# A second normalized-token tile in the router's stage of a two-layer encoder

## The chip, the cores and the metric

The kernel runs on one core of a Trainium2 chip. Its time is the device time of one execution in microseconds (us); smaller is better. The core's engines are named as the profile names them: PE (matrix multiply), DVE (vector), ACT (activations), POOL (general), and SP, which here only issues DMAs. DMAs that SP and ACT issue run on the same 16 DMA engines.

## The reference

Two layers over 512 tokens of 1,024 features. A layer is a mixer (a short convolution in the first, a gated linear recurrence in the second), a mixture of 32 experts with two experts for each token, and a gated embedding. Cut to what the change touches:

```python
h = h + mix                                    # the mixer's output projection ends here
xn = rmsnorm(h, norm_ffn[i])                   # y * g, y = h * rsqrt(mean(h*h) + EPS)
h = h + hier_moe(xn, ...)
# hier_moe:
pg = softmax(xn @ w_rg + b_rg); g_top = argmax(pg)          # 4 groups
le = (xn @ w_re + b_re) of the group g_top                  # 8 experts each
top_p, top_i = top_k(softmax(le), 2)                        # 2 experts a token
y = sum over the token's experts of weight * (silu(x @ w_gate[e]) * (x @ w_up[e])) @ w_down[e]
```

## The kernel before

Tokens lie in four tiles t = 0..3 of 128. Everything is built in an order written out by hand: each engine runs its instructions in the order in which the code issues them, and waits only for semaphores. A small queue, `Flow`, holds functions that are due some ticks later; the loops over the matrix multiplies tick it, so the router's steps for a tile are laid between the multiplies of the following tiles.

The mixer ends with `out_proj`, which finishes the tiles in the order 0 to 3. For each, `to_moe` adds the projection to `h` (L1323), and queues: the transposes for the router (`turn`, L762), its logits (L771), `norm`, `rest`, `ranks` and `weights`, and last `pull`. The steps that matter here:

- `norm(t)` makes the normalized tokens `xn` in two DVE instructions (L473); ACT copies them into the high part `X.hi` (L1336) and issues the write of `xn` to the DRAM table `xs` (L1337, 512 KB), from which later expert pairs gather rows.
- `rest(t)` makes the low part `X.lo` (L1341, DVE, two instructions, tile `x_z`).
- `ranks(t)` counts a token's place in its expert (PE L800 and L801, DVE L802), and DVE marks the places of the first four experts in `R` (L834, `hot`).
- `pull(t, p)` multiplies `R` with the high (p = 0) or low (p = 1) part (PE L830, eight matmuls each), and so gathers the tokens of the first four experts.

The four results of the pulls are copied to `xt` (ACT L944, DVE L942), and `gate_up(0)` starts the experts (PE L985). `leave` then frees the tiles of `X`, which become homes of weight loads. `Loader` issues all weight loads on SP in the order of use (L73), each as soon as a home is free; an expert's gate and up weights come in loads of 512 KB, its down weights in loads of 1 MB, 384 MB in both layers. A plain DMA's end is counted on one of eight semaphores (DMAHW0 to DMAHW7), and a new DMA on a semaphore waits until the last one there has ended.

The tile `xn` comes from the pool `bnd`, which is open while `out_proj` runs. The number of buffers is `bnd["xn"]`, 1 here. With one buffer, `norm(t)` must wait until the write of tile t - 1 to `xs` has read it to its end. When `bnd` closes, the space goes to `xt` and the experts' small tiles.

Of the kernel before, what the change touches and what calls it, by code (L numbers as in the profile page):

```python
# [10 lines left out]
F32 = mybir.dt.float32  # L11
F32R = mybir.dt.float32r
BF = mybir.dt.bfloat16
F16 = mybir.dt.float16
# [3 lines left out]
ALU = mybir.AluOpType  # L18
# [3 lines left out]
P = 128  # L22
# [3 lines left out]
KD = D // P  # L26
NG = 4
EPG = 8
NE = NG * EPG
# [4 lines left out]
OB = 128  # L34
# [195 lines left out]
def hybrid_encoder(ctx, tc, A, out):  # L230
    nc = tc.nc
    ctx.enter_context(tc.manual_schedule())

    def pool(name, bufs=1, side=None):
        return tc.tile_pool(name=name, bufs=bufs, side=side, reuse_waits="tile")
# [3 lines left out]
    bnd = {}  # L239
    small = ctx.enter_context(pool("small", 2))  # L240

    def homes(p, n, tag):
        return [(p, "%s%d" % (tag, j)) for j in range(n)]

    base = homes(ctx.enter_context(pool("base")), BASE, "base")
# [5 lines left out]
    def aux(shape, dt=F32):  # L251
        return psum.tile(shape, dt, name="aux", tag="aux", bufs=3)
# [116 lines left out]
    def iota(name, shape, dt=F32, **kw):  # L369
        t = const.tile(shape, dt, name=name)  # L370
        early.append(lambda: nc.gpsimd.iota(t, allow_small_or_imprecise_dtypes=True, **kw))
        return t
# [4 lines left out]
    nc.vector.memset(mhalf, -0.5)  # L377
    minus = const.tile([P, 1], F32, name="minus")
    nc.vector.memset(minus, -1.0)
    slot1 = iota("slot1", [P, OB], pattern=[[1, OB]], base=1, channel_multiplier=0)  # L380
    tok1 = iota("tok1", [P, S], F16, pattern=[[1, S]], base=-AWAY, channel_multiplier=0)
    tokp = iota("tokp", [P, T], pattern=[[P, T]], base=-AWAY, channel_multiplier=1)
    ovi = iota("ovi", [P, NOV], pattern=[[1, NOV]], base=0, channel_multiplier=0)
# [13 lines left out]
    gffn = [chan[:, P + i * KD:P + (i + 1) * KD] for i in range(2)]  # L397
# [163 lines left out]
    def out_proj(after):  # L561
        pss = [acc([P, 512]) for _ in range(T)]
        for j in range(4):
            wh, wl = W.take()
            for t in range(T):
                for kk in range(2):
                    k = 2 * j + kk
                    three(pss[t], X.h(t, k), X.l(t, k), wh[:, kk], wl[:, kk], k == 0, k == KD - 1)
                flow.tick()
            W.done()  # L570
            W.pump()
        for t in range(T):
            after(t, 0, pss[t])
        ws = [W.take() for _ in range(4)]
        for t in range(T):
            ps = acc([P, 512])
            token_group(ps, t, ws, lambda: after(t, 1, ps))
        W.done(4)

    def out_stage(i, Z, old, start, after):  # L580
        nonlocal X
        X = Z
        spare = bnd["spare"] = ExitStack()
        L.open(homes(spare.enter_context(pool("spare", 1, "right" if i else "left")), 1, "spare"), moe_end[i] + 4)
        with pool("bnd", 1, "right") as bnd["pool"]:
            bnd["xn"] = 1
            start()
            W.widen(old)
            spent = []

            def spend(at):
                if at in old:
                    return
                spent.append(at)
                L.open([at], moe_end[i] - 4 if len(spent) < WSP else None)

            W.spent = spend
            out_proj(after)
            assert len(spent) == WSP
            flow.drain()  # L600

    def mix_a(start, after):
        Z = Split(zhome)
        with pool("mixt", 2, "right") as mt:
            for q in range(4):
# [18 lines left out]
                for j in range(2):  # L624
# [4 lines left out]
                    split_z(Z, u, ft)  # L629
                    W.pump()  # L630
        out_stage(0, Z, xhome, start, after)
        xst.close()

    def mix_b(start, after):
# [91 lines left out]
        for ft in range(KD):  # L726
# [5 lines left out]
            W.pump()  # L732
        hs.close()
        out_stage(1, Z, zhome, start, after)
        zst.close()

    def router_load(i):
        wr = bnd["pool"].tile([P, KD, 40], F32, name="wr", tag="wr", bufs=1)
        st = bnd["pool"].tile([P, KD * 36], F32, name="wrs", tag="wrs", bufs=1)
        gv, ev = [st[:, a:b].rearrange("p (k g) -> p k g", k=KD) for a, b in ((0, KD * 4), (KD * 4, KD * 36))]  # L740
        nc.gpsimd.dma_start(gv, A["w_router_group"][i].rearrange("(k p) g -> p k g", p=P))
        nc.gpsimd.dma_start(ev, A["w_router_expert"][i].rearrange("(k p) g -> p k g", p=P))
        nc.vector.memset(wr[:, :, 4:8], 0.0)
        nc.vector.tensor_tensor(wr[:, :, :4], gv, gffn[i][:, :, None].to_broadcast([P, KD, 4]), op=ALU.mult)
        nc.vector.tensor_tensor(wr[:, :, 8:], ev, gffn[i][:, :, None].to_broadcast([P, KD, NE]), op=ALU.mult)
        rb = bnd["pool"].tile([P, 40], F32, name="rb", tag="rb", bufs=1)
        nc.vector.memset(rb[:, 4:8], -1e30)
        nc.gpsimd.dma_start(rb[:, :4], A["b_router_group"][i:i + 1].to_broadcast([P, 4]))
        nc.gpsimd.dma_start(rb[:, 8:], A["b_router_expert"][i:i + 1].to_broadcast([P, NE]))
        nc.vector.memset(les, -1e30)  # L750
        return wr, rb

    class Router:
# [12 lines left out]
        def logits(self, t, n, rs=None):  # L766
            v, g = nc.vector, nc.gpsimd
            ps = aux([P, 40])
            x = self.half.pop(t)
            for k in range(4):  # L770
                nc.tensor.matmul(ps, x[:, k], self.wr[:, 4 * n + k], start=(k == 0), stop=(k == 3))  # L771
            if n == 0:
                self.lgs[t] = small.tile([P, 40], F32, name="lg", tag="lg", bufs=5)
                v.tensor_copy(self.lgs[t], ps)
                return
            lg = self.lgs[t]
            v.tensor_tensor(lg, ps, lg, op=ALU.add)
            v.scalar_tensor_tensor(lg, lg, rs, self.rb, op0=ALU.mult, op1=ALU.add)
            m = small.tile([P, 2, 8], F32, name="rm", tag="rm", bufs=3)
            ix = small.tile([P, 2, 8], U32, name="rix", tag="rix")  # L780
            og = small.tile([P, NG], U32, name="og", tag="og")
            oh = small.tile([P, 2, NE], F32, name="oh", tag="oh", bufs=4)
            s = small.tile([P, 16], F32, name="rsc", tag="rsc", bufs=4)
            v.max(m[:, 0], lg[:, :8])
            v.max_index(ix[:, 0], m[:, 0], lg[:, :8])
            v.tensor_tensor(og, eidx[:, :NG], ix[:, 0, 0:1].to_broadcast([P, NG]), op=ALU.is_equal)
            le = les[:, t]
            v.copy_predicated(le.rearrange("p (g e) -> p g e", g=NG), og[:, :, None].to_broadcast([P, NG, EPG]),
                              lg[:, 8:].rearrange("p (g e) -> p g e", g=NG))
            v.max(m[:, 1], le)  # L790
            v.max_index(ix[:, 1], m[:, 1], le)
            v.tensor_tensor(oh, eidx[:, None, :].to_broadcast([P, 2, NE]), ix[:, 1, 0:2, None].to_broadcast([P, 2, NE]), op=ALU.is_equal)
            v.tensor_tensor(ohs[:, t], oh[:, 0], oh[:, 1], op=ALU.add)
            self.keep[t] = (oh, s, m, lg)
# [517 lines left out]
    for i in range(2):  # L1312
# [3 lines left out]
        def start():  # L1316
            box["g"] = gain(A["norm_ffn"][i])
            box["r"] = Router(*router_load(i))
# [128 lines left out]
```

## Time and profile before

| | us |
|---|---|
| median of 3 runs | 1540.57 |
| the undisturbed runs of these | 1539.45, 1540.57 |
| the profiled execution | 1539.66 |
| its span on the core | 1538.0 |
| PE busy | 1423.3 |
| DVE busy | 660.0 |
| ACT busy | 385.8 |
| POOL busy | 198.4 |

The profiled execution's time is 1.66 us over its span, and 0.91 us under the median of the runs. One run of the three was disturbed (2408.37 us) and is left out of all that follows. Times in the views are in us from the start of the span; L1337 is line 1337 of the kernel before. [...]

### The profile page before, as it was taken

How to read it: one execution, taken by the hardware profiler on the slowest of the kernel's cores; microseconds unless marked ns; L12 is line 12 of the kernel's file. 1: busy time of each engine (PE TensorE's matmuls, PEld its weight loads, DVE VectorE, ACT ScalarE, POOL GpSimd, SP SyncE). 2: the span in 40 equal slices, each digit the busy share in tenths (PEclk: the TensorE clock that was granted, in tenths of full speed). 3: DMA queues.
4: the chain of work that ended last, by engine and by line, in shares of the span. 5: the costliest groups of instructions: out<-in, count | busy, mean ns of one | idle time of the engine just before them, and what ended most of it. 6: DMA issues, size and time to landing. Idle time of an engine off the chain costs nothing. (4 is left out here: it accounts for less than half of the span.)

```text
span 1538.0 us, 17929 instructions
## 1 busy us (share of the span) xinstructions
PE 1423.3 (93%) x6774; PEld 808.3 (53%) x6774; DVE 660.0 (43%) x1157; ACT 385.8 (25%) x698; POOL 198.4 (13%) x295
## 2 busy tenths in 40 slices
PE   6999969999988999989999989799999889999897
PEld 5888853434333444336776658644343334443366
DVE  5544362434322333227756774624333223332275
ACT  4222321111101111005456754311111011111053
POOL 3300041000000000001233441310000000000011
PEclk9999999999999999999999999899999999999999
DMA  9423549999999999997222237499999999999941
GB/s 304 140 83 110 219 165 384 412 413 411 406 412 410 412 409 411 410 414 275 72 83 84 81 110 264 165 375 412 414 412 405 412 410 411 409 409 411 414 189 55
DMA packets 135279, 468.78 MB, mean 305 GB/s; under 512 B 14219, under 2 KB 39003, under 8 KB 118804
## 3 DMA queue, kind: packets, MB, share of 16 engines
q1 hardware_dynamic: 128036, 450.22, 75.0%
q0 software_dynamic: 5856, 12.90, 2.5%
q10 hardware_dynamic: 1296, 4.46, 0.7%
q8 instruction: 56, 0.92, 0.2%
q14 instruction: 35, 0.29, 0.1%
HBM read 468.59 MB, written 6.29 MB: 309 GB/s over the span
## 5 line engine op out<-in xcount | busy, mean ns | idle before, releaser
L991 DVE TENSOR_TENSOR hh<-acc,sl 128x256 f32<-128x256 f32 x64 | 39.6, 619 | 421.5 <-ACT sl L989 421.5
L866 DVE TENSOR_TENSOR h<-acc,h 128x512 f32<-128x512 f32 x224 | 140.9, 682 | 27.3 <-PE acc L864 26.9
L989 ACT ACTIVATE sl<-acc 128x256 f32<-128x256 f32 x64 | 24.6, 384 | 449.7 <-PE acc L985 449.7
L1011 PE MATMUL acc<-slot_base,ht 128*64 128x512 f32 x456 | 137.2, 594 | 0.1
L985 PE MATMUL acc<-slot_base,xt_base 128*64 128x512 f32 x544 | 123.1, 594 | 7.9 <-DMA slot_base<-in_w_exp_up_dram 7.9
L874 DVE SCALAR_TENSOR_TENSOR y_base<-acc,ws,y_base 128x512 fp32r<-128x512 f32 x64 | 48.1, 751 | 185.4 <-ACT y_base L873 181.4
L1105 POOL DMA_INDIRECT rows_z<-xs,ix x28 | 29.0, 1035 | 690.9 <-DVE marks L968 386.3
L873 ACT ACTIVATE y_base<-acc,ws 128x512 fp32r<-128x512 f32 x64 | 44.0, 687 | 266.8 <-PE acc L1011 252.0
L985 PE MATMUL acc<-slot_base,xt_xt 128*64 128x512 f32 x440 | 101.5, 595 | 7.3 <-DMA slot_base<-in_w_exp_up_dram 7.2
L1011 PE MATMUL acc<-slot_z,ht 128*64 128x512 f32 x344 | 98.1, 607 | 0.0
L863 PE MATMUL acc<-y_base,marks 128*128 128x512 f32 x224 | 95.0, 424 | 0.0
L864 PE MATMUL acc<-y_base,marks 128*128 128x512 f32 x224 | 88.3, 394 | 0.0
L985 PEld LDWEIGHTS acc<-slot_base,xt_base 128*64 128x64 f32 x544 | 38.9, 137 | 89.3 <-issue 85.2
L498 PE MATMUL acc<-x_x,pair_base 128*128 128x512 f32 (+1 forms) x208 | 78.4, 377 | 1.0 <-DVE x_x L486 1.0
L497 PE MATMUL acc<-x_x,pair_base 128*128 128x512 f32 (+1 forms) x208 | 78.6, 378 | 0.0
L499 PE MATMUL acc<-x_x,pair_base 128*128 128x512 f32 (+1 forms) x208 | 78.2, 376 | 0.0
L497 PE MATMUL acc<-pair_base,x_z 128*128 128x512 f32 (+1 forms) x164 | 66.1, 403 | 5.8 <-ACT pair_base L149 5.3
L1011 PEld LDWEIGHTS acc<-slot_base,ht 128*64 128x64 f32 x456 | 43.3, 137 | 50.3 <-issue 46.2
L985 PEld LDWEIGHTS acc<-slot_base,xt_xt 128*64 128x64 f32 x440 | 31.7, 137 | 72.0 <-issue 64.1
L498 PE MATMUL acc<-pair_base,x_z 128*128 128x512 f32 (+1 forms) x164 | 65.2, 398 | 0.5 <-DVE pair_base L160 0.5
L499 PE MATMUL acc<-pair_base,x_z 128*128 128x512 f32 (+1 forms) x164 | 64.8, 395 | 0.7 <-DVE x_z L494 0.7
L1011 PEld LDWEIGHTS acc<-slot_z,ht 128*64 128x64 f32 x344 | 29.2, 139 | 58.7 <-issue 49.6
(294 smaller groups left out, 2624.7 us busy)
## 6 DMA issues: line engine op xcount, KB each, us to landing
slot_base<-in_w_exp_gate_dram SPq DMA_DIRECT2D x123, 512.0 KB
slot_base<-in_w_exp_up_dram SPq DMA_DIRECT2D x123, 512.0 KB
slot_base<-in_w_exp_down_dram SPq DMA_DIRECT2D x57, 1024.0 KB
slot_z<-in_w_exp_down_dram SPq DMA_DIRECT2D x43, 1024.0 KB
slot_late<-in_w_exp_gate_dram SPq DMA_DIRECT2D x44, 512.0 KB
slot_late<-in_w_exp_up_dram SPq DMA_DIRECT2D x44, 512.0 KB
slot_z<-in_w_exp_gate_dram SPq DMA_DIRECT2D x36, 512.0 KB
slot_z<-in_w_exp_up_dram SPq DMA_DIRECT2D x36, 512.0 KB
```

What stands on the lines that cost most here:

```text
L497: nc.tensor.matmul(ps, lh, rh, start=first, stop=False)
L498: nc.tensor.matmul(ps, lh, rl, start=False, stop=False)
L499: nc.tensor.matmul(ps, ll, rh, start=False, stop=last)
L863: nc.tensor.matmul(ps, sg[:, t * P:(t + 1) * P], yh[:, n * 512:(n + 1) * 512], start=True, stop=False)
L864: nc.tensor.matmul(ps, sg[:, t * P:(t + 1) * P], yl[:, n * 512:(n + 1) * 512], start=False, stop=True)
L866: nc.vector.tensor_tensor(hv, ps, hv, op=ALU.add)
L873: nc.scalar.activation(yh[:, sl], yps[n], AF.Copy, scale=ws)
L874: nc.vector.scalar_tensor_tensor(yl[:, sl], yps[n], ws, yh[:, sl], op0=ALU.mult, op1=ALU.subtract)
L985: nc.tensor.matmul(ps[hf * C:(hf + 1) * C].rearrange("p (g f) -> p g f", g=2), xt[:, k, lo:lo + C], rv[:, :, kk, hf * 256:(hf + 1) * 256], ...
L991: nc.vector.tensor_tensor(hh.rearrange("p j q -> p q j"), ps[:, 256:].rearrange("p (q j) -> p q j", j=2), sl.rearrange("p (q j) -> p q j", ...
L1011: nc.tensor.matmul(yps[n][a * C:(a + 1) * C], hts[a][:, j, half], rv[:, j, n * 512:(n + 1) * 512], start=(half == 0 and j == 0), stop=(hal ...
L1105: nc.gpsimd.indirect_dma_start(out=xg.rearrange("p k q -> p (k q)"), out_offset=None, in_=xs[i], in_offset=bass.IndirectOffsetOnAxis(ap=ix ...
```

## The change

Five edits. The pool `bnd` gets two buffers for `xn` in this stage. To make room for the 4,096 bytes per partition, the tile `wrs` (1,152 bytes), into which the router's weights were loaded before they were scaled into `wr`, is dropped: they are loaded into `wr` and scaled in place. The table `slot1` becomes 16-bit floats (256 bytes less), `lg` has 4 buffers and not 5 (160 bytes less), `oh` 3 and not 4 (256 bytes less).

```diff
-    slot1 = iota("slot1", [P, OB], pattern=[[1, OB]], base=1, channel_multiplier=0)
+    slot1 = iota("slot1", [P, OB], F16, pattern=[[1, OB]], base=1, channel_multiplier=0)
...
-            bnd["xn"] = 1
+            bnd["xn"] = 2
...
         wr = bnd["pool"].tile([P, KD, 40], F32, name="wr", tag="wr", bufs=1)
-        st = bnd["pool"].tile([P, KD * 36], F32, name="wrs", tag="wrs", bufs=1)
-        gv, ev = [st[:, a:b].rearrange("p (k g) -> p k g", k=KD) for a, b in ((0, KD * 4), (KD * 4, KD * 36))]
+        gv, ev = wr[:, :, :4], wr[:, :, 8:]
         nc.gpsimd.dma_start(gv, A["w_router_group"][i].rearrange("(k p) g -> p k g", p=P))
         nc.gpsimd.dma_start(ev, A["w_router_expert"][i].rearrange("(k p) g -> p k g", p=P))
         nc.vector.memset(wr[:, :, 4:8], 0.0)
-        nc.vector.tensor_tensor(wr[:, :, :4], gv, gffn[i][:, :, None].to_broadcast([P, KD, 4]), op=ALU.mult)
-        nc.vector.tensor_tensor(wr[:, :, 8:], ev, gffn[i][:, :, None].to_broadcast([P, KD, NE]), op=ALU.mult)
+        nc.vector.tensor_tensor(gv, gv, gffn[i][:, :, None].to_broadcast([P, KD, 4]), op=ALU.mult)
+        nc.vector.tensor_tensor(ev, ev, gffn[i][:, :, None].to_broadcast([P, KD, NE]), op=ALU.mult)
...
-                self.lgs[t] = small.tile([P, 40], F32, name="lg", tag="lg", bufs=5)
+                self.lgs[t] = small.tile([P, 40], F32, name="lg", tag="lg", bufs=4)
...
-            oh = small.tile([P, 2, NE], F32, name="oh", tag="oh", bufs=4)
+            oh = small.tile([P, 2, NE], F32, name="oh", tag="oh", bufs=3)
```

No instruction is added, dropped or moved on any engine; the lines behind L738 stand one line earlier. What changes is what instructions wait for, and where tiles lie. DVE in the first layer, from `norm(2)` to `ranks(2)`, before (`x_z` is the low part, the two L473 rows behind it are `norm(3)`):

```order
L473 SCALAR_TENSOR_TENSOR xn<-h,ss,gain 128x512 [waits DMAHW2_49]
L473 SCALAR_TENSOR_TENSOR xn<-h,ss,gain 128x512
L1323 TENSOR_TENSOR h<-acc,h 128x512 [waits PE_49]
L1341 TENSOR_TENSOR x_z_399<-xn,x_z_397 128x512 [waits Activation_49]
L1341 TENSOR_TENSOR x_z_400<-xn,x_z_398 128x512 [waits Activation_49]
L473 SCALAR_TENSOR_TENSOR xn<-h,ss,gain 128x512 [waits DMAHW4_49,DVE_49,Pool_49]
L473 SCALAR_TENSOR_TENSOR xn<-h,ss,gain 128x512
L802 SCALAR_TENSOR_TENSOR rk<-aux,ohs 128x32 [waits PE_49]
L834 TENSOR_TENSOR R_146<-slot_133,rk 128x256 [waits DVE_49]
```

The same place on DVE after the change:

```order
L473 SCALAR_TENSOR_TENSOR xn<-h,ss,gain 128x512 [waits DMAHW1_49]
L473 SCALAR_TENSOR_TENSOR xn<-h,ss,gain 128x512
L1322 TENSOR_TENSOR h<-acc,h 128x512 [waits PE_49]
L1340 TENSOR_TENSOR x_z_399<-xn,x_z_397 128x512 [waits Activation_49]
L1340 TENSOR_TENSOR x_z_400<-xn,x_z_398 128x512 [waits Activation_49]
L473 SCALAR_TENSOR_TENSOR xn<-h,ss,gain 128x512 [waits DMAHW2_49,DVE_49,Pool_49]
L473 SCALAR_TENSOR_TENSOR xn<-h,ss,gain 128x512
L801 SCALAR_TENSOR_TENSOR rk<-aux,ohs 128x32 [waits PE_49]
L833 TENSOR_TENSOR R_146<-slot_133,rk 128x256 [waits DVE_49]
```

The writes of tiles 0, 1 and 2 are counted on DMAHW1, DMAHW2 and DMAHW4. So `norm(3)` waited for the write of tile 2 and now waits for that of tile 1, and `norm(2)` for that of tile 0 in place of tile 1.

ACT in the first layer, from `norm(3)`'s copies to the first copy of a pull's result, before:

```order
L1336 CAST x_z_397<-xn 128x512 [waits DVE_49]
L1336 CAST x_z_398<-xn 128x512 [waits DVE_49]
L1337 DMA xs_74<-xn 128x1024 [waits DMAHW1_49]
L811 ACTIVATE rsc<-lg,rsc 128x4 [waits Pool_49]
L812 ACTIVATE rsc<-rm 128x1
L811 ACTIVATE rsc<-lg,rsc 128x4 [waits Pool_49]
L812 ACTIVATE rsc<-rm 128x1 [waits DVE_49]
L944 COPY xt_xt_1818<-acc 128x512 [waits DMASW4_49,DMASW3_49,DMAHW1_49,DMASW2_49,DMAHW2_49,DMASW1_49,DMAHW4_49,DVE_49,PE_49]
```

And after:

```order
L1335 CAST x_z_397<-xn 128x512 [waits DVE_49]
L1335 CAST x_z_398<-xn 128x512 [waits DVE_49]
L1336 DMA xs_74<-xn 128x1024 [waits DMAHW0_49]
L810 ACTIVATE rsc<-lg,rsc 128x4 [waits Pool_49]
L811 ACTIVATE rsc<-rm 128x1
L810 ACTIVATE rsc<-lg,rsc 128x4 [waits Pool_49]
L811 ACTIVATE rsc<-rm 128x1 [waits DVE_49]
L943 COPY xt_xt_1817<-acc 128x512 [waits DMAHW1_49,DMAHW2_49,DMAHW0_49,DMAHW4_49,DVE_49,PE_49]
```

The write of tile 3 is counted on DMAHW1 before and on DMAHW0 after, so it now waits for the load that used DMAHW0 last (the down weights in `slot_base`) and not for the write of tile 0. The copy to `xt` waits for all four writes before and after, since `xt` lies in the space of `bnd`; in the second layer this copy waits for none of them in either kernel. The first DMA of this stage on POOL (`gain`) waits, after the change, also for the loads of small tables at the kernel's start.

Where tiles lie, read from the two built programs: the buffers on the left side of SBUF, `base` among them, start 672 bytes lower. All 384 MB of expert weights go to buffers that start 224 bytes past a multiple of 256 before; after, 269 MB of them go to buffers that start 64 bytes past one, and 115 MB to buffers that have not moved. The residual tile `h` starts 32 bytes past one before.

## Rows read from the trace of the kernel before

**Rows 1.** Page, part 2: DMA engines' busy tenths in 40 slices of the span.

```profile
DMA  9423549999999999997222237499999999999941
```

**Rows 2.** Windows inside the two expert stages: PE busy, DVE, ACT, POOL; then PEclk, DMA share, GB/s.

```profile
300.00:400.00 100.00, 98.00 (x471) 40.83 (x471) 35.50 (x71) 11.89 (x24) 4.79 (x6) 1.00 1.02 409
1100.00:1200.00 100.00, 96.08 (x456) 39.10 (x452) 33.24 (x68) 11.89 (x24) 4.69 (x5) 1.00 1.02 409
```

**Rows 3.** Waits of DVE, whole span: total us, times, longest.

```profile
DVE xn L473 <- DMA xs<-xn: 13.9, 3, 7.8
```

**Rows 4.** Timeline, first layer: start, us, engine; in brackets idle before, and releaser.

```profile
211.93 0.33 ACTq L1337 DMA_DIRECT2D xs<-xn  x1
...
213.82 0.57 POOL L463 TENSOR_TENSOR ss<-ss,mhalf 128x1 f32<-128x1 f32 x1
...
221.41 0.33 SPq L73 DMA_DIRECT2D slot_more<-in_w_exp_up_dram  x1
221.51 2.20 DVE L473 SCALAR_TENSOR_TENSOR xn<-h,ss,gain 128x512 f32<-128x512 f32 x2 [7.83 <-DMA xs<-xn]
...
223.75 0.33 ACTq L1337 DMA_DIRECT2D xs<-xn  x1
...
224.33 3.45 PE L830 MATMUL acc<-R,x_z 128*128 128x256 f32 x16 [8.15 <-DVE R L834]
...
226.41 0.21 DVE L793 TENSOR_TENSOR ohs<-oh 128x32 bf16<-128x32 f32 x1
...
227.62 0.24 PE L800 MATMUL aux<-ohs,ones 128*128 128x32 bf16 x3
...
229.21 1.28 DVE L1341 TENSOR_TENSOR x_z<-xn,x_z 128x512 fp32r<-128x512 f32 x2
...
230.56 0.33 SPq L73 DMA_DIRECT2D slot_z<-in_w_exp_gate_dram  x1
230.57 1.10 ACT L944 COPY xt_xt<-acc 128x512 f32<-128x512 f32 x2 [1.64 <-PE acc L830]
...
231.22 5.37 PE L985 MATMUL acc<-slot_base,xt_xt 128*64 128x512 f32 x24
```

**Rows 5.** Windows of the same place in the first layer; columns as in Rows 2.

```profile
221.40:227.10 5.70, 2.77 (x13) 2.77 (x14) 4.76 (x16) 1.72 (x5) 1.93 (x6) 0.50 0.80 315
227.10:231.30 4.20, 3.43 (x31) 2.91 (x32) 3.07 (x8) 1.30 (x5) 3.03 (x10) 0.99 0.00 0
```

**Rows 6.** Timeline, second layer.

```profile
980.46 2.08 PE L830 MATMUL acc<-R,x_z 128*128 128x256 f32 x16
...
981.41 2.33 DVE L473 SCALAR_TENSOR_TENSOR xn<-h,ss,gain 128x512 f32<-128x512 f32 x2 [1.05 <-DMA xs<-xn]
...
985.67 0.58 POOL L463 TENSOR_TENSOR ss<-ss,mhalf 128x1 f32<-128x1 f32 x1
...
990.58 2.18 DVE L473 SCALAR_TENSOR_TENSOR xn<-h,ss,gain 128x512 f32<-128x512 f32 x2 [5.04 <-DMA xs<-xn]
...
993.38 3.78 PE L830 MATMUL acc<-R,x_z 128*128 128x256 f32 x16 [2.96 <-DVE R L834]
...
1000.21 0.33 SPq L73 DMA_DIRECT2D slot_z<-in_w_exp_gate_dram  x1
```

**Rows 7.** Windows of the same place in the second layer.

```profile
990.00:1001.20 11.20, 7.50 (x40) 7.04 (x40) 7.38 (x24) 2.85 (x9) 5.65 (x18) 0.50 0.29 98
```

**Rows 8.** DMA queues, 212 to 216 and 216 to 220: packets, MB, share of 16 engines.

```profile
q1 hardware_dynamic: 250, 0.91, 90.3%
...
q1 hardware_dynamic: 311, 1.13, 69.6%
q10 hardware_dynamic: 135, 0.50, 31.6%
```

**Rows 9.** DMA queues, 3.0 to 3.5 (loads of `h`) and 310 to 340.

```profile
q1 hardware_dynamic: 50, 0.19, 94.5%
...
q1 hardware_dynamic: 2801, 12.00, 99.3%
```

## The prediction

> **What bounds the kernel now.** I read the page's DMA line first. Twice it stands at 9 for 12 slices in a row, 24 slices of 38.45 us, so some 920 us of the 1,538 are the two expert stages [rows 1]. Inside them the DMA engines are busy at a share of 1.02 and move 409 GB/s, while PE, though 96 to 98% busy, has idle time left [rows 2]: the stages run at the pace of the weight loads. In such a stage time is gained only where the DMA engines stood idle or could have begun earlier. Then I read DVE's waits: the normalization L473 waited three times for the write to `xs`, 13.9 us in all, 7.8 at most [rows 3]. The question is how much of these 13.9 us lies on the way to the first experts, and whether the loads come earlier too.
>
> In the first layer the two timelines of `norm(3)` and of its write answer it [rows 4]. The write of tile 2 is issued at 211.93. The scale for tile 3 is ready at 213.82 + 0.57 = 214.39. DVE stands idle for 7.83 us and begins `norm(3)` at 221.51, when that write has landed. Nothing else in the queue of DVE can pass it: `ranks(2)`, the marks L834 and the logits of tile 3 stand behind it, PE waits 8.15 us for the marks, and then come the pulls, `rest(3)` at 229.21, the copies to `xt` at 230.57 and the first expert at 231.22. SP, which waits for the tiles of `X`, issues its next load at 230.56. Meanwhile the DMA engines are at a share of 0.80 from 221.4 to 227.1 and at 0.00 from 227.1 to 231.3 [rows 5]. So the wait is on the path, and it costs the loads too. In the second layer the same wait is 5.04 us at 990.58, and `norm(2)` has one of 1.05 us at 981.41; SP's next load comes at 1000.21 [rows 6]; from 990 to 1001.2 the DMA share is 0.29 [rows 7].
>
> **The change, part by part.** Two buffers of `xn`. In the first layer `norm(3)` now waits for the write of tile 1, and in before `norm(2)`, two normalizations earlier in time than 214.39, had already waited for that one, so it is done. What is late next is the scale: start at about 214.45 in place of 221.51, so 7.06 us earlier. All that follows on DVE moves with it: the logits of tile 3 end at 226.41 + 0.21 - 7.06 = 219.56. On PE two further things shrink. The 16 pulls of tile 2 took 3.45 us at a granted clock of 0.50 [rows 4, 5], against 2.08 for 16 at 1.00 [rows 6]; PE sat idle for 8.15 us before them, and without the wait for 8.15 - 7.06 = 1.1 us, so I take the full clock. The count L800 came only when these pulls were over, at 227.62, one microsecond after its operand; it now comes at about 219.6, 8.0 us earlier. `rest(3)` and SP's next load follow it, 8.0 us earlier, at 221.2 and 222.5.
>
> The copies to `xt` need one more thing: they wait for all four writes to `xs`, since they overwrite the pool's space. Before, the write of tile 3 (issued at 223.75) was in time for 230.57. Now it is issued at 223.75 - 7.06 = 216.7, behind the loads and the write of tile 2 that SP and ACT had issued until then. The trace shows what such a write meets: that of tile 2 moved no packet until 216 (its queue, q10, is missing from 212 to 216 and has a third of the packets from 216 to 220 [rows 8]) and took 221.41 - 211.93 = 9.5 us, as SP's wait for the same write shows [rows 4]. [...] The landing is bounded from both sides: not felt at all (copies at 230.57 - 8.0 = 222.6), or 9.5 us as for tile 2 (226.2). I take 224.5: after tile 2's landing at 221.4, a load and this write remain, 1.05 MB at 409 GB/s [rows 2] or 2.6 us, and half a microsecond for the end. So the experts start 6.1 us earlier, between 4.4 and 8.0.
>
> For the loads the gain is the idle share that is filled. SP's next load is issued at 222.5, while the engines still work off what was issued before (they were at 0.80 up to 227.1), so from then on they don't stop. The idle time was 0.20 x 5.7 = 1.1 us and 4.2 us [rows 5], 5.3 in all. The loads set the stage, and PE's 6.1 us cover them: **5.3 us** for the first layer.
>
> In the second layer `norm(2)` starts 1.05 us earlier. That moves the residual of tile 3, its sum of squares and its scale: 985.67 + 0.58 - 1.05 = 985.2. `norm(3)` starts at 985.25 and not at 990.58, 5.33 us earlier [rows 6]. The loads issued before are few here, the DMA engines are idle for 0.71 x 11.2 = 8.0 us from 990 to 1001.2 [rows 7], so all of SP's advance counts. No copy to `xt` waits for a write in this layer. The clock is the open part: it is 0.50 in all of this stretch [rows 7], the pulls of tile 2 take 3.78 us and not 2.08 [rows 6]. If it stays at 0.50 the gain is 5.33. If it stays at 1.00 the count behind the pulls comes some 1.3 us earlier still, as `rest(3)` and SP's load do: 6.6. PE's idle times ahead of the pulls shrink by the same waits of 1.05 and 5.04 us, so I take the better half, **6.1 us**.
>
> The other edits. Loading the router's weights straight into `wr` leaves the same DMAs and the same two multiplies; they stand before the projection's end, and DVE has idle time there. The marks with a 16-bit table stand twice on the path of each layer. `ranks(2)` and its marks together took the time from the end of `norm(3)`, 223.71, to the pulls at 224.33, 0.62 us; if the type slowed or sped the marks by a half, that would be at most 0.6 us a layer either way. I take zero. Fewer buffers of `lg` and `oh` add no wait to any instruction in the built program. POOL's `gain` waits for loads that have ended long ago. The write of tile 3 now waits for the semaphore of a load; before, SP had already issued its next load on that semaphore by the time of the write of tile 2, so that one has ended: zero.
>
> Sum: 5.3 + 6.1 = 11.4 us. From the profiled 1539.66 that gives 1528.3; the median of before lies 0.9 higher, and I forecast its counterpart, **1529 us**, 0.7% less. A measurement of this kernel can tell about 2% from no change, so this counts as the same.
>
> **Rivals.** First, *the gain stays in the stage*. The experts start earlier, but with less of their weights loaded, and PE waits for loads instead. For it speaks that the stage runs at the loads' pace [rows 2]; against it, that the loads start earlier too, since SP waits for the same `rest(3)`. It decides if a later wait on a slot, not the idle time of 227 to 231, sets when the stream is full. Then half the gain or less is left: 1535 to 1541.
>
> Second, *the moved buffers cost*: slower than before. 70% of the expert weights (269 of 384 MB) now go to buffers that start elsewhere within 256 bytes. If a packet takes 1% longer there, the two stages lose 0.70 x 920 x 1% = 6.4 us, so from 1.8% on the gain is eaten. The nearest rows are the loads of `h`, which start at 32 and not at 224: 0.945 x 8 / 0.19 = 39.8 engine-us per MB, against 0.993 x 480 / 12.00 = 39.7 for the bulk [rows 9]. That says no difference, but 0.19 is rounded by up to 2.6%, so up to 17 us either way are not excluded: 1546 at worst.
>
> Third, the same place with the other sign: *a better start within 256 bytes*, with 17 us less by the same rows, 1512, and more if 64 is better than 32 by itself. [...]
>
> **How the numbers follow.** My forecast, 9.7 to 14.6 us of gain with the bounds above (4.4 + 5.3 up to 8.0 + 6.6), holds 1526 to 1531, and 1 to 2 us of scatter between executions on either side; chance 0.80. The gain that stays in the stage 0.09, slower buffers 0.05, better buffers 0.05, the rest 0.01. The range of 1523 to 1538 takes in the forecast with its scatter and the near half of the first rival. Over 2% faster would need 1509.8 or less, which only the third rival gives, by half of its chance: 0.03. Over 2% slower needs 1571: 0.01. The rest, 0.96, is within 2%.
>
> **What would show it.** In the profile after: no DVE wait of L473 for `xs` in either layer; the pulls of tile 2 in the first layer right after the scale, at a clock of 1.00 and 2.1 us long; SP's `slot_z` load some 8 us earlier there and 5 to 7 in the second layer; copies to `xt` that wait for the write in the first layer, for about 2 us; no stretch of idle DMA engines between 222 and 232. The stages that follow should be as long as before, with 1.02 and 409 GB/s. I am wrong if the DMA rate in the expert stages moves, if the first expert starts early and the stage's end does not, or if the write of tile 3 lands after 226.

## The result, and the profile after

| | before | after |
|---|---|---|
| median of the undisturbed runs, us | 1540.93 (4 runs, 1539.45 to 1541.8) | 1533.95 (5 runs, 1531.22 to 1534.62) |
| profiled execution, us | 1539.66 | 1534.22 |
| its span, us | 1538.0 | 1532.5 |

Single executions were disturbed (2408.37 us beside the kernel before, later 1819.65 in e3 and 2071.33 beside e5 to e8) and are left out of all medians. The ratio is 0.9944, with a 95% interval of 0.9930 to 0.9957: about 0.6% less, 7.0 us by the medians and 8.6 by the ratio, inside the 2% that count as no change here. The forecast was 1529 with a range of 1523 to 1538; of the 11.4 us that it summed up, 7.0 are there by the medians.

The page's DMA line, which answers [rows 1], has the same shape, with 12 full slices in the first layer and 12 in the second:

```profile
DMA  9423649999999999997222237599999999999941
```

The waits of DVE after (total us, times, longest) have one row for L473. It has no wait for `xs` any more, against three in [rows 3]; what is left is the scale from POOL:

```profile
DVE xn L473 <- POOL ss L463: 12.2, 7, 5.8
```

The timeline of the first layer after, to be laid beside [rows 4] (start, us, engine; in brackets idle before, and releaser). Lines from 739 on stand one earlier than before:

```profile
216.09 0.33 ACTq L1336 DMA_DIRECT2D xs<-xn  x1
...
217.98 0.57 POOL L463 TENSOR_TENSOR ss<-ss,mhalf 128x1 f32<-128x1 f32 x1
...
218.59 2.30 DVE L473 SCALAR_TENSOR_TENSOR xn<-h,ss,gain 128x512 f32<-128x512 f32 x2 [0.74 <-POOL ss L463]
...
220.94 0.33 ACTq L1336 DMA_DIRECT2D xs<-xn  x1
...
221.51 2.18 PE L829 MATMUL acc<-R,x_z 128*128 128x256 f32 x16 [1.18 <-DVE R L833]
...
225.22 0.33 SPq L73 DMA_DIRECT2D slot_more<-in_w_exp_up_dram  x1
225.35 1.29 DVE L1340 TENSOR_TENSOR x_z<-xn,x_z 128x512 fp32r<-128x512 f32 x2
...
226.70 0.33 SPq L73 DMA_DIRECT2D slot_z<-in_w_exp_gate_dram  x1
...
229.11 1.07 ACT L943 COPY xt_xt<-acc 128x512 f32<-128x512 f32 x2 [2.38 <-issue]
229.16 1.29 DVE L941 COPY xt_xt<-acc 128x512 f32<-128x512 f32 x2 [2.52 <-DMA xs<-xn]
...
229.75 6.70 PE L984 MATMUL acc<-slot_base,xt_xt 128*64 128x512 f32 x24 [2.32 <-ACT xt_xt L943]
```

Three things are to be seen. First, the stage does what was forecast: `norm(3)` starts 0.61 us after the scale began and not 7.69; the pulls of tile 2 take 2.18 us and not 3.45; SP's `slot_z` load follows `norm(3)` by 8.1 us where the pulls at half clock had made it 9.05. Second, the whole stage comes too late. The write of tile 2 is issued at 216.09, before at 211.93: 4.16 us were lost ahead of the place that the change is about. Third, and not in the forecast, PE waits 2.32 us for the copies to `xt`, and the granted clock falls after it (0.63 in the last window below). The first 24 expert products take 6.70 us and not the 5.37 of [rows 4].

The windows of this place after (PE, weight loads, DVE, ACT, POOL; then PEclk, DMA share, GB/s). Against [rows 5] the stretch without DMA traffic is gone:

```profile
222.00:225.00 3.00, 2.18 (x24) 1.99 (x23) 2.42 (x14) 0.02 (x1) 2.50 (x8) 1.00 1.02 408
225.00:228.00 3.00, 2.39 (x16) 1.92 (x16) 1.64 (x4) 0.57 (x3) 2.02 (x6) 1.00 1.02 418
228.00:232.00 4.00, 2.25 (x6) 0.77 (x8) 1.29 (x2) 2.36 (x3) 3.38 (x7) 0.63 1.03 383
```

The second layer after, timeline, and the window that answers to [rows 7]:

```profile
983.67 0.57 POOL L463 TENSOR_TENSOR ss<-ss,mhalf 128x1 f32<-128x1 f32 x1
...
990.57 2.56 PE L829 MATMUL acc<-R,x_z 128*128 128x256 f32 x16 [0.73 <-DVE R L833]
...
992.40 0.33 SPq L73 DMA_DIRECT2D slot_z<-in_w_exp_gate_dram  x1
...
993.06 1.94 PE L984 MATMUL acc<-slot_base,xt_xt 128*64 128x512 f32 x8
```

```profile
983.00:993.00 10.00, 7.95 (x68) 7.16 (x66) 8.35 (x25) 3.53 (x13) 5.09 (x15) 1.00 0.83 265
```

SP's load comes 7.8 us earlier than in [rows 6], of which 1.0 is there already when this layer's mixing stage ends; the clock is 1.00 throughout, and the DMA engines are at 0.83 in place of 0.29.

**Where the 4 us go.** Matrix products of the first layer's mixing stage between 40 and 160 us, before and then after (count; busy us, mean ns of one; idle before):

```profile
L498 PE MATMUL acc<-x_x,pair_base 128*128 128x512 f32 x168 | 65.4, 389 | 0.0
L499 PE MATMUL acc<-x_x,pair_base 128*128 128x512 f32 x168 | 65.4, 389 | 0.0
L497 PE MATMUL acc<-x_x,pair_base 128*128 128x512 f32 x167 | 65.0, 389 | 0.0
L497 PE MATMUL acc<-pair_base,x_z 128*128 128x512 f32 x10 | 3.9, 389 | 0.0
L498 PE MATMUL acc<-pair_base,x_z 128*128 128x512 f32 x9 | 3.5, 389 | 0.0
L499 PE MATMUL acc<-pair_base,x_z 128*128 128x512 f32 x9 | 3.5, 389 | 0.0
```

```profile
L499 PE MATMUL acc<-x_x,pair_base 128*128 128x512 f32 x168 | 66.6, 397 | 0.0
L498 PE MATMUL acc<-x_x,pair_base 128*128 128x512 f32 x168 | 66.6, 397 | 0.0
L497 PE MATMUL acc<-x_x,pair_base 128*128 128x512 f32 x167 | 66.2, 397 | 0.0
L497 PE MATMUL acc<-pair_base,x_z 128*128 128x512 f32 x4 | 1.6, 390 | 0.0
L499 PE MATMUL acc<-pair_base,x_z 128*128 128x512 f32 x4 | 1.6, 390 | 0.0
L498 PE MATMUL acc<-pair_base,x_z 128*128 128x512 f32 x4 | 1.6, 389 | 0.0
```

PE is never idle in this stretch and the clock is 1.00 in both, yet 531 products fit into 120 us before and 515 after: 226 and 233 ns each, 7 ns more. (The mean of one is longer than this distance because the records of neighbours overlap: before, the 531 add up to 206.7 us in the 120.) The first layer has 528 products of this form, 3.7 us. The last product of line L497 in the mixing stage, which stands for the end of that stage in all that follows, ends at 209.3 us before and at 213.5 after. No instruction was added on PE; what changed for these products is where `pair_base` lies, 672 bytes lower, while `x_x`, on the right side of SBUF, has not moved. Why this should matter no view says, so the experiments begin there.

### The profile page after: what moved, and what is told of

The parts are those of the page before. It is cut to its first block, busy times and chain, and to the rows that moved or that the text cites. A ratio compares the mean times of both kernels' runs of the same rounds, so it can differ in the third digit from the quotient of the medians.

```text
span 1532.5 us, 17933 instructions
## 1 busy us (share of the span) xinstructions
PE 1424.2 (93%) x6774; PEld 802.6 (52%) x6774; DVE 660.8 (43%) x1157; ACT 385.4 (25%) x698; POOL 197.7 (13%) x295
## 5 line engine op out<-in xcount | busy, mean ns | idle before, releaser
L498 PE MATMUL acc<-x_x,pair_base 128*128 128x512 f32 (+1 forms) x208 | 80.0, 385 | 1.0 <-DVE x_x L486 1.0
L497 PE MATMUL acc<-x_x,pair_base 128*128 128x512 f32 (+1 forms) x208 | 80.2, 386 | 0.0
L499 PE MATMUL acc<-x_x,pair_base 128*128 128x512 f32 (+1 forms) x208 | 79.9, 384 | 0.0
L497 PE MATMUL acc<-pair_base,x_z 128*128 128x512 f32 (+1 forms) x164 | 65.9, 402 | 5.4 <-ACT pair_base L149 5.3
```

What stands on the lines that cost most here:

```text
L497: nc.tensor.matmul(ps, lh, rh, start=first, stop=False)
L498: nc.tensor.matmul(ps, lh, rl, start=False, stop=False)
L499: nc.tensor.matmul(ps, ll, rh, start=False, stop=last)
```

## The experiments

Each was timed in turn with the kernel before, except those marked "one execution". In the table of stages, "to the experts" is the time from the end of the mixing stage to the first expert product, and "experts" from there to the last product that sums the experts' results (`marks` with `y_base`).

### The edits and the second tile apart

The changed kernel with the old number of tiles in both layers, or in one:

```diff
-            bnd["xn"] = 2
+            bnd["xn"] = 1                      # e1_space_only
+            bnd["xn"] = 2 if i == 0 else 1     # e2_first_layer_only
+            bnd["xn"] = 2 if i == 1 else 1     # e3_second_layer_only
```

> The changed kernel with one tile of normalized tokens in the router's stage, so that only the edits that give the space are left. Theory: the second tile makes the whole gain, and the products of the first layer's mixing stage, which ran at 397 ns each after the change instead of 389, are slowed by the moved addresses; then this kernel shows 397 ns there and takes 1541.3 + 4.2 = 1545.5 us (1544 to 1547). Rival A: the pace of those products differs from one execution to the next whatever the addresses; then the time is that of the kernel before, 1540 to 1542, and the trace may show either 389 or 397. Rival B: the edits themselves gain something; then it is below 1538.

> The changed kernel with two tiles in the first layer's router stage and one in the second's. Theory: the second tile is worth 5.7 to 6.2 us in the first layer by its trace (start and end of the expert stage against the end of the mixing products), and the addresses cost 4.2: 1541.3 - 6 + 4.2 = 1539.5 (1538 to 1541). Rival A (addresses cost nothing): 1535.3. Rival B (the gain is given back in the expert stage): no less than 1541.

> The changed kernel with one tile in the first layer's router stage and two in the second's. Theory: 5.1 us from the second layer and 4.2 lost in the first: 1541.3 - 5.1 + 4.2 = 1540.4 (1539 to 1542). Rival A (addresses cost nothing): 1536.2. In the second layer the experts' first product should start 7 to 8 us after slot_more's load as in the changed kernel, with the clock at 1.00 throughout.

And the kernel before, unchanged, one execution:

> The kernel before, once more, for its trace. Theory (addresses set the pace of the first layer's mixing products): 389 ns each again, the end of these products at 209.3 us after the start within 0.5. Rival A (executions differ): another mean, up to 397 ns.

| kernel | us, median | ratio to before, 95% | `x_x` products, ns | second tile is worth |
|---|---|---|---|---|
| e1_space_only | 1545.02 | 1.0031 [1.0019, 1.0043] | 396 | |
| e2_first_layer_only | 1539.46 | 0.9984 [0.9976, 0.9993] | 396 | 1545.02 - 1539.46 = 5.6 |
| e3_second_layer_only | 1539.93 | 0.9991 [0.9983, 1.0000] | 396 | 1545.02 - 1539.93 = 5.1 |
| before, beside them | 1541.56 | | 389 (e4, again) | |

The three came out within 0.5 us of the theory, and both rivals fall. The space edits alone make the kernel 3.5 us slower. The second tile is worth 5.6 and 5.1 us, 10.7 together, and 1545.02 - 10.7 = 1534.3 is the changed kernel. The intervals leave each of these worths open by some 2 us: by the ratios they are 7.2 and 6.2. In e3 the clock is 1.00 from 985 to 999 us, as expected; its first expert product follows the last load of `slot_more` by 3.9 us and not by 7 to 8, and the changed kernel has 3.2 there, so that part of the expectation was wrong. Four executions at the new addresses had 396 to 397 ns, two at the old ones 389: it isn't a difference between executions. For e1 the same view as above:

```profile
L498 PE MATMUL acc<-x_x,pair_base 128*128 128x512 f32 x168 | 66.6, 396 | 0.0
L499 PE MATMUL acc<-x_x,pair_base 128*128 128x512 f32 x168 | 66.6, 396 | 0.0
```

### Is it the address?

Unused bytes ahead of the large buffers on the left side, in the kernel before (32 and 64) and in e1 (32):

```diff
     small = ctx.enter_context(pool("small", 2))
+    nc.vector.memset(small.tile([P, 8], F32, name="pad", tag="pad", bufs=1), 0.0)    # 8: 32 bytes, 16: 64
```

and in the changed kernel 32 bytes less, by one tile for two constants:

```diff
-    mhalf = const.tile([P, 1], F32, name="mhalf")
+    powers = const.tile([P, 2], F32, name="powers")
+    mhalf, minus = powers[:, :1], powers[:, 1:]
     nc.vector.memset(mhalf, -0.5)
-    minus = const.tile([P, 1], F32, name="minus")
```

> The kernel before with 32 unused bytes ahead of the large buffers of the left side, so that base and what follows start 32 bytes higher (pair_base from byte 89,312 to 89,344), while x_x on the right stays at 180,192. Theory (a product is slower when its two operands start at different places within 64 bytes; before, both stood at byte 32 of 64, now one at 0 and one at 32): the first layer's mixing products at 396 ns in place of 389, the time 1541.5 + 3.5 to 4.2 = 1545 to 1546. Rival (it is not the place but something else in the space edits): 389 ns and 1541.5.

> The same with 64 bytes (pair_base at 89,376, byte 32 of 64 as x_x, but byte 32 of 256 where x_x has 224). Theory (within 64 bytes): 389 ns, the time of before, 1540 to 1542. Rival (within 128 or 256 bytes): 396 ns, 1545.

> The space edits alone (one tile of normalized tokens in both layers), with 32 unused bytes ahead of base: pair_base at 88,672, byte 32 of 64, 96 of 256. Theory (within 64 bytes): 389 ns and 1541.5, the space edits cost nothing by themselves. Rival (within 256 bytes): 396 ns and 1545. Rival (the edits cost by themselves, for instance by the fewer buffers of the router's small tiles): 389 ns and over 1543.

> The changed kernel with the two one-column constants of the powers in one tile, which takes 32 bytes less, so that all large buffers of the left side start 32 bytes lower (pair_base at 88,608, byte 32 of 64). Theory: the second tile keeps its 10.5 us and the products run at 389 ns: 1541.5 - 10.5 = 1531, or 1534 - 4 = 1530 (1528.5 to 1531.5). Rival (within 128 or 256 bytes): 1534, that of the changed kernel.

| kernel | left buffers start at, mod 256 | `x_x` products, ns | GB/s, 300 to 400 and 1100 to 1200 | us |
|---|---|---|---|---|
| before | 224 | 389 | 409, 409 | 1541.47 |
| changed | 64 | 397 | 410, 410 | 1533.95 |
| e5_before_pad_32 | 0 | 396 | 418, 420 | 1526.51, ratio 0.9898 [0.9883, 0.9913] |
| e6_before_pad_64 (one execution) | 32 | 396 | 410, 409 | 1545.77 |
| e7_space_pad_32 | 96 | 395 | 410, 410 | 1545.43, ratio 1.0023 [1.0014, 1.0032] |
| e8_two_tiles_32_less | 32 | 396 | 410, 410 | 1531.52, ratio 0.9936 [0.9923, 0.9950] |

The right side starts at 224 in all of them. It is the address: 32 bytes of padding in the kernel before, with the one `memset` that writes them, bring the slow products. But "within 64 bytes" is wrong, since byte 32 and byte 96 stand at the same byte of 64 as 224 does and are slow. Only 224 beside 224 is fast. e8's time, 1531.52, lies at the edge of the range that was expected with fast products, but its products are slow; its ratio and that of the changed kernel (0.9944) lie in each other's interval, so the two are the same.

And e5 shows what no theory had expected of it: slow products, and yet 15.0 us gained. Its windows inside the two expert stages:

```profile
300.00:400.00 100.00, 98.17 (x477) 42.98 (x478) 38.30 (x79) 13.13 (x27) 5.60 (x6) 1.00 1.02 418
1100.00:1200.00 100.00, 95.39 (x452) 38.89 (x450) 31.97 (x65) 11.90 (x24) 4.69 (x5) 1.00 1.02 420
```

The changed kernel in the same windows:

```profile
300.00:400.00 100.00, 98.63 (x475) 41.33 (x475) 35.39 (x71) 11.88 (x24) 4.65 (x6) 1.00 1.02 410
1100.00:1200.00 100.00, 92.29 (x434) 37.52 (x432) 29.90 (x62) 10.51 (x22) 4.67 (x5) 1.00 1.02 410
```

The same share of 1.02 moves 418 to 420 GB/s in e5 where before moved 409 [rows 2]. So the loads are faster in the one kernel of the table whose left buffers start at a multiple of 256, and 32, 64, 96 and 224 are alike, with 409 to 410. In the trace's packet records a 4-KB packet takes 160.0 ns on average in e5 and 163.84 in before (stretch of 300 to 700 us), 2.3% less. A start at 64 does no better than one at 224: after the change it is 163.8 ns. Why the multiple of 256 is faster no view says.

### Both places at once

Three tests of the two rules: 64 bytes less in the changed kernel, so that only the left side starts at a multiple of 256; both sides there, without and with the second tile; both sides at byte 32.

```diff
-            s = small.tile([P, 16], F32, name="rsc", tag="rsc", bufs=4)    # e9, e11: 64 bytes less
+            s = small.tile([P, 16], F32, name="rsc", tag="rsc", bufs=3)
...
-            oh = small.tile([P, 2, NE], F32, name="oh", tag="oh", bufs=3)  # e11: 256 bytes less
+            oh = small.tile([P, 2, NE], F32, name="oh", tag="oh", bufs=2)
...
+    nc.vector.memset(ctx.enter_context(pool("edge", 1, "right")).tile([P, 56], F32, name="edge"), 0.0)
     early_ring = open_early(0)                                             # e10, e11: 224 bytes; e12: 192
```

e10 and e12 also have the padding on the left, 32 and 64 bytes.

> The changed kernel with three instead of four buffers of the router's small tile rsc, 64 bytes less, so that base and all that follows on the left start 64 bytes lower (pair_base at 88,576, a multiple of 256). Theory (a load's packets take 160.0 ns in place of 163.8 when the buffer that they are written to starts at a multiple of 256 bytes, as the run of before with 32 bytes of padding showed; that run gained 15.1 us though its mixing products ran at 396 ns, about 4 us lost, so the packets are worth 19 us): 1534 - 19 = 1515 (1513 to 1518), loads at 418 to 420 GB/s, mixing products still at 396 ns. Rival (the run with the padding gained by something other than the start of its buffers): 1534.

> The kernel before with 32 unused bytes ahead of base and 224 unused bytes at the right edge, so that the large buffers on both sides start at multiples of 256. Theory (mixing products run at 389 ns when both operands start at the same byte of 256, loads faster where their buffer starts at a multiple of 256): 1541.6 - 19 for the 269 of 384 MB of the experts' weights that go to the left, - 8 for the 115 MB that go to the right = 1514.5 (1511 to 1518), products at 389 ns. Rival (the pace of the products belongs to the place of before, not to equal places): 396 ns and 1518.5. Rival (the experts' stages become bound by TensorE first): less gain, over 1518, with the loads' rate below 420 GB/s.

> The changed kernel with rsc in three and oh in two buffers, 320 bytes less, and 224 unused bytes at the right edge: all large buffers at multiples of 256. Theory: the second tile's 10.5 us and the places' 27 add up, 1541.6 - 27 - 10.5 = 1504 (1500 to 1508). Rival (with faster loads the experts' stages are bound by TensorE, and the earlier loads are worth nothing): that of before with all buffers at multiples of 256, 1514.

> The kernel before with 64 unused bytes ahead of base and 192 at the right edge: large buffers on both sides at byte 32 of 256. Theory (equal places within 256 bytes give the products 389 ns, only multiples of 256 give faster loads): 389 ns, loads as before at 409 GB/s, 1540 to 1542. Rival (the products' pace hangs on the place itself and not on both being equal): 395 to 396 ns, 1545.

| kernel | left, right, mod 256 | tiles | `x_x` products, ns | GB/s | us | ratio to before, 95% |
|---|---|---|---|---|---|---|
| e9_two_tiles_64_less | 0, 224 | 2 | 396 | 419, 418 | 1515.35 | 0.9827 [0.9814, 0.9840] |
| e10_before_all_256 | 0, 0 | 1 | 389 | 421, 421 | 1518.62 | 0.9855 [0.9840, 0.9870] |
| e11_two_tiles_all_256 | 0, 0 | 2 | 389 | 421, 421 | 1505.63 | 0.9772 [0.9759, 0.9785] |
| e12_before_all_32 (one execution) | 32, 32 | 1 | 389 | 409, 409 | 1538.83 | |

e9 fell on the theory's number. It has the instructions of the changed kernel, with one buffer of `rsc` less, and its large left-hand buffers lie 64 bytes lower: 18.6 us. e12 tells the two rules apart: with both sides at byte 32 the products are fast and the loads are not. e11 has both gains, at 1505.63 inside its range, and is the fastest kernel here, 36 us under the one before. The products of e10, in the same view:

```profile
L501 PE MATMUL acc<-x_x,pair_base 128*128 128x512 f32 x168 | 65.4, 389 | 0.0
L500 PE MATMUL acc<-x_x,pair_base 128*128 128x512 f32 x168 | 65.4, 389 | 0.0
L499 PE MATMUL acc<-x_x,pair_base 128*128 128x512 f32 x167 | 65.0, 389 | 0.0
```

Two numbers missed. e12's one execution is 1.2 us under its 1540 to 1542, which no run explains. e10 is 4 us over its 1514.5. From e5 to e10 the products give back 3.9 us (the mixing stage ends at 213.1 and at 209.2), so the right-hand buffers are worth 7.9 - 3.9 = 4 us and not 8, and from e9 to e11 again 9.7 - 5.5 = 4.2. By the expert stages of the table below it is 5.6 and 6.1. Whether the 115 MB that go to the right gain less for each MB than the 269 on the left, or the 8 was an overestimate, is open. The rival that the stages become bound by TensorE is not what e10 shows: the loads run at 421 GB/s in both windows, the DMA engines are at 1.02 as before, and PE still has idle time (98.6 and 97.0 us busy of 100, where the kernel before had 98.0 and 96.1 [rows 2]).

```profile
300.00:400.00 100.00, 98.63 (x475) 41.42 (x475) 35.84 (x72) 11.88 (x24) 5.10 (x6) 1.00 1.02 421
1100.00:1200.00 100.00, 97.01 (x466) 42.15 (x464) 36.05 (x74) 12.12 (x26) 5.71 (x6) 1.00 1.02 421
```

The stages of the profiled executions, in us:

| kernel | mixing 1 ends | to the experts 1 | experts 1 | to the experts 2 | experts 2 |
|---|---|---|---|---|---|
| before | 209.3 | 21.9 | 492.8 | 21.6 | 491.9 |
| e1_space_only | 213.6 | 23.7 | 491.2 | 20.5 | 492.3 |
| e2_first_layer_only | 213.5 | 15.8 | 492.9 | 20.4 | 492.7 |
| e3_second_layer_only | 213.9 | 23.6 | 491.4 | 14.1 | 492.5 |
| changed | 213.5 | 16.2 | 492.3 | 13.8 | 494.5 |
| e5_before_pad_32 | 213.1 | 22.5 | 483.6 | 20.6 | 486.3 |
| e8_two_tiles_32_less | 212.4 | 15.7 | 492.6 | 14.0 | 493.1 |
| e9_two_tiles_64_less | 214.6 | 15.7 | 484.0 | 13.8 | 485.6 |
| e10_before_all_256 | 209.2 | 22.3 | 482.1 | 20.4 | 482.1 |
| e11_two_tiles_all_256 | 209.1 | 16.0 | 481.3 | 14.0 | 482.2 |

## Why the prediction was right, and where it fell short

The time lies in the range, and the mechanism is the one forecast. One step failed: the sum has no term for the moved buffers. "The other edits" puts the rest of the change at zero, and only the second and third rival price the addresses, in the loads alone. They cost 3.5 us (e1), in the products of the first layer's mixing stage, which the prediction did not speak of. 11.4 - 3.5 = 7.9 is close to the 7.0 measured. That the time is in the range is in part luck: 1533.95 is beyond the 1526 to 1531, with 1 to 2 us of scatter, to which the forecast gave 0.80, and in the room that was left for the first rival. And 64 bytes of address that no one chose decide between 1533.95 and e9's 1515.35, which is outside it.

**The first layer.** Forecast 5.3 us for the loads under PE's 6.1; measured 5.6 by the medians and 7.2 by the ratios (e2). Counted from the end of the mixing stage, since that end moved by 4.2: SP's `slot_z` load came at 230.56 - 209.3 = 21.3 before and 226.70 - 213.5 = 13.2 after, 8.1 earlier (forecast 8.0). The experts started 21.9 - 16.2 = 5.7 earlier (forecast 6.1, bounds 4.4 and 8.0). This close agreement is in part luck. At the same addresses it is 23.7 - 15.8 = 7.9 (e1, e2), because one-tile kernels differ here: in e1 the pulls of tile 2 and of tile 3 both ran slowly, the window from 221 to 237 has a granted clock of 0.62, and the pulls of tile 3 took 3.75 us where the kernel before had 2.56.

```profile
228.84 3.79 PE L829 MATMUL acc<-R,x_z 128*128 128x256 f32 x16 [8.54 <-DVE R L833]
233.60 3.75 PE L829 MATMUL acc<-R,x_z 128*128 128x256 f32 x16 [0.73 <-DVE R L833]
```

The copies to `xt` waited for the write of tile 3 as said, 2.52 us at 229.16 (forecast about 2). That write took from 220.94 to about 229.1, 8.2 us, near the 9.5 of tile 2's in [rows 4] and the 224.5 - 216.7 = 7.8 of the forecast. Its last packet ended at 228.54, 0.57 before the copy at 229.11, which is the half microsecond that the forecast had for the end; before, tile 2's last packet ended at 220.95, 0.56 ahead of `norm(3)`. The pulls at full clock, 2.18, were right to 0.1.

**The second layer.** Forecast 6.1 us, measured 5.1 by the medians and 6.2 by the ratios (e3), too coarse to choose between the two values weighed there (5.33 and 6.6). The clock stayed at 1.00, which was the condition of the 6.6. Against the kernel before the experts started 21.6 - 13.8 = 7.8 us earlier, but 1.2 of these are there in e1 without a second tile; at the same addresses it is 20.5 - 14.1 = 6.4 (e1, e3) and 6.7 (e1, changed). In the changed kernel's profiled execution the expert stage then took 494.5 us and not 491.9, as if the first rival gave a part back. The other traces speak against it: with two tiles e3 has 492.5 and e8 493.1, and one-tile kernels without faster loads have 491.6 to 492.8. From e1 to e3 6.2 of the 6.4 us are left at the end of the stage, as "all of SP's advance counts" said. So the 2.6 us look like scatter of one execution and not like a gain given back; a further profile of the changed kernel would have to show it.

**The moved buffers.** The second and third rivals asked whether a start at 64 makes a 4-KB packet dearer or cheaper than one at 224. It does neither: 163.8 ns in both, 409 and 410 GB/s. The row of the loads of `h` at 32 had said no difference, and that was so: 32, 64, 96 and 224 are alike (409 to 410 GB/s), and only the multiple of 256 is not (418 to 420 in e5). No row of the kernel before that the prediction used has a buffer there. With it the third rival's sign and its size of 17 us would have come true: e9 is 18.6 us under the changed kernel. What the forecast needs beside these 17 us for a time under 1509.8, that 64 beats 32 by itself, no run shows: the changed kernel (64) and e8 (32) both move 410 GB/s.

**The other terms.** The 16-bit marks cost nothing that shows: L833 takes 0.42 us, as L834 did. Fewer buffers of `lg` and `oh` brought no wait.

## What to carry to other kernels

Free space by a multiple of 256 bytes, or check where the large buffers start after it: a small table that shrinks moves all that lies behind it, and here that took back a third of the second tile's 10.7 us, and a start 64 bytes lower would have brought 18.6. Where loads set the pace, as they do here, try buffers at multiples of 256 first: with both sides there the kernel before took 1518.62 us (e10), and with both at 224 it took 1542.01 beside it. To price an edit that also moves addresses, run the moved addresses alone.

## What the runs showed that was not expected

- Products of an operand on the left with one on the right ran at 389 ns (mean record) when both buffers started at the same byte of 256 (224 and 224, 32 and 32, 0 and 0) and at 395 to 397 when they did not (0, 32, 64 or 96 on the left with 224 on the right). It costs about 7 ns a product, at the same granted clock (1.00 from 40 to 160 us, before and after) and with no idle time. Products of two left-hand operands, `x_z` with `pair_base`, ran at 389 to 390 in either case on the second and third of their lines, and at 406 to 407 on the first in every kernel. An exception stays unexplained: two of the three lines of the second layer's output products, `pair_z` with `x_z`, ran at 391 to 393 with 32 on the left and 224 on the right (e6, e8), as fast as before, and at 394 to 397 with 0, 64 and 96. What in the chip makes the 7 ns is open.
- 4-KB weight loads into buffers that start at a multiple of 256 bytes took 160.0 to 160.1 ns a packet (mean of the records from 300 to 700 us) with the left side there (e5, e9) and 159.4 to 159.5 with both (e10, e11), against 163.7 to 163.8 at the four other starts (32, 64, 96 and 224). In the expert stages that made 418 to 421 GB/s in place of 409 to 410 at the same DMA share of 1.02.
